# Grouping small float32 products by array shape in a two-block kernel on one core

## The chip, the cores and the metric

The kernel runs on one core of a Trainium2 chip. Its engines are TensorE (PE in the profile, with PEld for its weight loads), VectorE (DVE), ScalarE (ACT), GpSimd (POOL) and SyncE (SP, which mostly issues transfers). The metric is device microseconds of one launch; the median of several runs counts.

## The reference

Two blocks on x of [1024 tokens, 1024 channels], all in float32. Block 1: a mixer (half pooling, half a state-space model), then a SwiGLU layer. Block 2: attention and a gated recurrence side by side, then a squared-ReLU layer and a gate. The change touches the two recurrences only:

```python
def ssm_mixer(u, ...):            # 32 groups of 16 channels, 64 complex states each
    bu_r = jnp.einsum('blgh,gph->blgp', ug, bbar_r)     # and bu_i
    _, _, s_r, s_i = lax.associative_scan(_complex_affine_combine, (a_r, a_i, bu_r, bu_i), axis=1)
    y = einsum('blgp,ghp->blgh', s_r, c_re) - einsum('blgp,ghp->blgh', s_i, c_im) + d_skip * ug
    ...
def wkv7_scan(r, decay, k, v, a_vec, b_vec):            # 8 heads, state 64x64 each
    def step(state, inp):
        sa = jnp.einsum('bhvk,bhk->bhv', state, a_t)
        state = (state * d_t[:, :, None, :] + sa[..., None] * b_t[:, :, None, :]
                 + v_t[..., None] * k_t[:, :, None, :])
        return state, jnp.einsum('bhvk,bhk->bhv', state, r_t)
```

## The kernel before, in words

Large products split each operand into two parts of reduced precision and add three matmuls (lines L139 to L141, tile `big`); they make up most of the program. The two recurrences use plain float32 matmuls on small tiles, each of which stands in the trace as two matmul instructions. The source order is a suggestion: the framework's scheduler reorders instructions by readiness under its own costs, and each engine then runs its list strictly in that order.

**State-space mixer (block 1, about 115 to 240 us).** Four blocks b of 8 groups, chunks of 8 tokens. `ssm_taps(b)` makes, for each group g, two products into `pk` with a stationary operand of 128 rows by 16 columns (L413 with `c0`, L414 with `ca`) and a 128 by 128 transpose of `w` into `pt` (L415). DVE makes `c0` (L405); ACT copies `pk` to `ks` and `pt` to `bct` (L416, L417). `ssm_states(b)` makes for each group one product with 128 stationary columns into `pa` (L436) and two with 64 columns into the halves of `pb` (L437, L438); DVE multiplies `pa` (L439), then `pb` (L440), and scans. On PE `ssm_taps(b + 1)` follows `ssm_states(b)` directly, so L413 waits there for DVE's L405, which stands behind L439, two residual additions (L542) and L440. Between the blocks stand 24 large matmuls (`part_resid`) and `ssm_out`. The pool of `big` tiles has four buffers.

**Recurrence of block 2 (about 1300 to 1810 us).** Four time blocks tb of four chunks of 64 tokens. `wkv_prep(tb)` makes what does not need the state, the last of it the pair products (L1111): per chunk four products for the even heads (partitions 0 to 63) into one PSUM bank, four for the odd ones (64 to 127) into the other; DVE masks each bank into `at` (L1112), and SP stores its diagonal blocks. The pool `ps` has two banks. `wkv_inverse(tb)` loads these blocks and inverts them on DVE in 248 small steps over the four time blocks (L1140, L1141), stores and reloads the result, and finishes with products on PE (L1164, L1170). `wkv_chain(tb)` takes the four chunks one after the other: L1189 and L1190 (into `px`), a copy, L1195 (into `pu`), two copies, L1201 (update of the state), then for each of 8 heads the output as a sum of two products in place: L1204 (128 rows by 64 columns) and L1205 (64 by 64). DVE adds L1201's result to the state (L1207, L1208), but waits for the whole tile, L1205 included; the next chunk's L1190 needs that state. `wkv_chain(tb - 1)` is interleaved with `wkv_prep(tb)` and both with `wkv_inverse`. Large matmuls of the gate projections fill PE between them. L1018 (part of `head_rnorm`) needs a reciprocal of DVE (L1012).

Of the kernel before, what the change touches and what calls it, by code (L numbers as in the profile page):

```python
# [48 lines left out]
class Kernel:  # L49
# [49 lines left out]
    def split(self, x, hi, lo, scale=None):  # L99
        """hi + lo = x (or scale * x) exactly, each part of float32r's precision"""  # L100
        nc = self.nc
        if scale is None:
            nc.scalar.copy(hi, x)  # L103
            nc.vector.tensor_tensor(lo, x, hi.bitcast(F32), ALU.subtract)  # L104
        else:
            nc.scalar.activation(hi, x, AF.Identity, scale=scale)
            nc.vector.scalar_tensor_tensor(lo, x, scale, hi.bitcast(F32), ALU.mult, ALU.subtract)

    def half_pair(self, name):
        """hi and lo of [128, 512] in one slot"""  # L110
        t = self.slot(name, F32R)
        return t[:, 0:H], t[:, H:2 * H]

    def split_halves(self, x, name, scale=None):
        """The two token halves of [128, 1024], each with hi and lo in a slot of its own"""
        nc = self.nc
        out = [self.half_pair(name) for _ in range(2)]
        xs = [x[:, half * H:half * H + H] for half in range(2)]
        if scale is None:
            scale = 1.0  # L120
        for (hi, lo), xh in zip(out, xs):
            nc.scalar.activation(hi, xh, AF.Identity, scale=scale)
        for (hi, lo), xh in zip(out, xs):
            nc.vector.scalar_tensor_tensor(lo, xh, scale, hi.bitcast(F32), ALU.mult, ALU.subtract)
        return out
# [49 lines left out]
    def scaled(self, tiles):  # L175
        """The tiles with their rows scaled to a mean square of 1"""
        ss, xs = self.sumsq(tiles)
        rs = self.rsqrt(ss, len(tiles), 1.0 / D, EPS)
        for i, x in enumerate(tiles):
            self.nc.vector.tensor_scalar(xs[i], x, rs[:, i:i + 1], None, ALU.mult)  # L180
        return xs

    def norm_t_half(self, xs, g, out):
        """out: for each channel tile the hi and lo [128, 512] of g * xs, transposed"""
# [14 lines left out]
    def norm_t(self, res, g, groups=(3, 1), scaled=None):  # L199
        """The normalised input and what fills one half of it; scaled: the tiles, scaled already"""  # L200
# [15 lines left out]
    def units_steps(self, ws, x, nk=NK, w_off=0):  # L216
        """For each w: out[ch 128, tok 1024]; w: hi/lo [128, nk * 128], x[k][half]: hi/lo [128, 512]; a step for each half"""
# [11 lines left out]
    def norm_units(self, norm_half, x, ws):  # L229
        """norm_half(half) fills x[k][half]; the first units run between the halves"""  # L230
# [11 lines left out]
    def tok_matmul(self, x, w, evac):  # L242
        """out[tok 128, 1024 cols], x[k][half]: hi/lo [ch, tok 512], w: list of row blocks hi/lo [ch, 1024]"""
# [33 lines left out]
    def turns(self, out, phi, n):  # L277
        """out = (phi mod 2 pi) / (2 pi) in [-0.5, 0.5]"""
# [92 lines left out]
    def ssm_maps(self, b):  # L371
        """Input and output maps and rotations of the 8 groups of block b, from the parameters alone"""
# [5 lines left out]
        # input maps abar^j bbar (of token 7 - j of a chunk) and output maps C abar^(j + 1)  # L378
# [7 lines left out]
        # rotation by the angle of the chunk  # L386
# [11 lines left out]
    def ssm_taps(self, b, maps):  # L398
# [10 lines left out]
        # taps K[h, g, (tau, h')] of the convolution inside a chunk  # L409
        pk, pt = self.big(), self.big()  # L410
        g8 = lambda q: q.rearrange("p (g c) -> p g c", g=8)
        for g in range(8):
            nc.tensor.matmul(pk[0:16, g * P:g * P + 16], lhsT=w[:, g, 0:16], rhs=c0[:, g, :], start=True, stop=True)  # L413
            nc.tensor.matmul(pk[0:16, g * P + 16:(g + 1) * P], lhsT=w[:, g, 0:16], rhs=ca[:, g, 0:112], start=True, stop=True)  # L414
            nc.tensor.transpose(pt[:, g * P:(g + 1) * P], w[:, g, :], self.ident)  # L415
# [10 lines left out]
    def ssm_states(self, b, prep, ut):  # L426
        """States of block b at the ends of the chunks: rotated, then a real scan"""
# [6 lines left out]
        for g in range(8):  # L434
            sl = slice(g * P, (g + 1) * P)
            nc.tensor.matmul(pa[:, sl], lhsT=bct[:, g, :], rhs=ut[:, g, :], start=True, stop=True)  # L436
            nc.tensor.matmul(pb[0:64, sl], lhsT=bct[:, g, 64:128], rhs=ut[:, g, :], start=True, stop=True)  # L437
# [15 lines left out]
    def ssm_out(self, b, prep, states):  # L453
        """[ch 128, tok 1024] of block b"""
# [22 lines left out]
    def ssm_inputs(self, ps, b):  # L477
        """u^T [(g, h), tok] of 8 groups to DRAM as [(g, h), (j, c)] for tokens 8 c + j"""
# [5 lines left out]
    def ssm_load(self, b):  # L484
        """[(j 8, h 16), g 8, c 128], token 7 - j of chunk c"""
# [7 lines left out]
    def pool_diff(self, gi, pu):  # L493
        """Mean of the window minus the token"""
# [27 lines left out]
    def part_resid(self, mix, w_rows, src, dst):  # L522
        """dst = src + mix^T @ w, in steps"""
# [97 lines left out]
    def row_blocks(self, w, k0, n=4):  # L621
        """n row blocks of w from k0 on"""
        return [self.weights(w[(k0 + k) * P:(k0 + k + 1) * P, :], keep=True) for k in range(n)]

    def resid_matmul(self, mix, w, res):
        """res += mix^T @ w"""
# [9 lines left out]
    def ffn(self, res, g, chunks, up, act, w_down, last=lambda: None):  # L636
        """last: what goes between the last products; up: arrays of the weights that a tile of the hidden layer needs; act: what makes the tile of their products"""
# [40 lines left out]
    def block1(self, x2):  # L678
        """The rows of x2 go to DRAM; returns the normalised input of block 2 and what fills one half of it"""
# [10 lines left out]
        def scaled(ts):  # L690
            """Rows of rmsnorm(res) * g to x2, then scaled for the next norm"""
# [22 lines left out]

    def rope_tables(self):
        """[cos, cos, -sin, sin] over the 32 + 32 rotary rows (twice), and [sin rows | cos rows] of the keys"""
# [20 lines left out]
    def latents(self, cl, rs, rt):  # L737
        """hi and lo [ch, tok] of the two latents from DRAM with the gains of their norms, and the factors of the norms,
        which the products with them get: [tok 128, 8 tiles] and [128, tok]"""
# [22 lines left out]
    def heads(self, hp, out, psum, cq, ckv, kpe, cs, rq, rk):  # L762
        """Queries (with the scale of the softmax in them) and keys of a pair of heads to out, in 6 steps"""
# [28 lines left out]
    def attention(self, cq, ckv, rv, rq, rk):  # L792
        """hi and lo of the outputs [ch, tok] of each pair of heads"""
# [90 lines left out]
    def rope_keys(self, hn, w):  # L884
        """The rotary part of the keys and the table of the queries, to DRAM"""
# [12 lines left out]
    def rwkv_z(self, norm_half, hn):  # L898
        """Token-shifted projections: r, k, v go to DRAM; the low-rank inputs stay on chip"""
# [51 lines left out]
    def rwkv(self, hn):  # L951
        nc, a = self.nc, self.a
        # the diagonal blocks [time block, pair of chunks, block, head parity, chunk, head pair, row, column], then their inverses
# [34 lines left out]
    def per_pt(self, out, x, func, scale=1.0, bias=0.0):  # L988
        """One activation for each of the four head pairs, with its own column of scale and bias"""
# [4 lines left out]
    def head_sum(self, x):  # L994
        """Sums over the channels of each head, on all of its channels, in two banks of 2 head pairs"""
# [7 lines left out]
    def head_rnorm(self, x, scale, bias, floor):  # L1003
        """1 / max(sqrt(scale * (sum over a head) + bias), floor), on all channels of the head, in two banks"""
# [23 lines left out]
    def wkv_prep(self, tb, live):  # L1028
        """What the chunks of time block tb need apart from the state, in steps"""
# [13 lines left out]
        # normalised removal key  # L1043
# [11 lines left out]
        # even heads lie on partitions 0..63, odd ones on 64..127; the products of a pair of chunks have the  # L1055
        # rows of k before those of b for even heads, after them for odd ones
# [19 lines left out]
        # bonus  # L1076
# [8 lines left out]
        # token-major values (their mean over the head removed) and keys, pair products of each chunk  # L1085
        mask = self.cst[:, 744:872].unsqueeze(1).to_broadcast([P, 4, P])
        brow = (od, ev)
        for c2 in range(2):
# [16 lines left out]
            for c in range(2):  # L1105
                c4 = 2 * c2 + c
                at.append(self.slot("at").rearrange("p (e a t) -> p e a t", e=2, a=4))
                for e, rows in enumerate((ev, od)):
                    ps = self.ps()
                    for pt in range(4):  # L1110
                        nc.tensor.matmul(ps[:, pt * P:(pt + 1) * P], lhsT=bk[c2][rows, c, pt, :, :], rhs=ar[c2][rows, c, pt, :, :], start=True, stop=True)  # L1111
                    nc.vector.tensor_tensor(at[c4][:, e], ps.rearrange("p (a t) -> p a t", a=4), mask, ALU.mult)  # L1112
# [6 lines left out]
    def wkv_inverse(self, tb, live):  # L1119
        """Inverses of the 32 x 32 diagonal blocks by substitution, then of the 64 x 64 ones"""  # L1120
        nc = self.nc
        ar, at, bt, uv, bv, dp = live
        # partitions: pair of chunks, parity r of the row, block, head parity, chunk, head pair; row 2 k + r lies at k
# [32 lines left out]
        # T21 = T22 A21 T11  # L1156
# [17 lines left out]
    def wkv_chain(self, live):  # L1174
        """The chunks of a time block one after the other, a step for each"""
# [7 lines left out]
        for c in range(4):  # L1183
# [16 lines left out]
            for pt, e in hs:  # L1200
                nc.tensor.matmul(pg[half[e], pt * 64:pt * 64 + 64], lhsT=bt[c // 2][:, c % 2, pt, half[e]], rhs=u4[:, pt, e, :], start=True, stop=True)  # L1201
            for pt, e in hs:
                o = pg[half[e], 256 + pt * 64:320 + pt * 64]
                nc.tensor.matmul(o, lhsT=u4[:, pt, e, :], rhs=at[c][:, e, pt, 64:128], start=True, stop=False)  # L1204
                nc.tensor.matmul(o, lhsT=self.state[half[e], pt, :], rhs=ars(pt, e, 1), start=False, stop=True)  # L1205
# [7 lines left out]
    def wkv_out(self, tb, live):  # L1213
        """Group norm, bonus, gate"""
# [16 lines left out]
    def projections(self, hn):  # L1231
        """The gates and the latents before their norm, to DRAM, and the factors of the norms: [tok 128, 8 tiles of each]
        and [8 tiles of each, tok 128]"""
# [31 lines left out]
    def branch(self, w, x, g0, other=None, step=lambda i: None):  # L1265
        """gate * (x @ w); with other, hi and lo of its sum with that; step(i): what goes ahead of unit i"""
# [24 lines left out]
    def ple_inputs(self):  # L1291
        """hi and lo of p, transposed, and of its weights"""
# [12 lines left out]
    def ple_proj(self):  # L1305
        """p @ w_ple_proj, to DRAM"""
# [73 lines left out]
def layout(i):  # L1380
    """The arrays of setup_inputs() in the order in which the kernel reads them."""
# [114 lines left out]
```

## Time and profile before

| what | value |
|---|---|
| runs: median (lowest to highest) | 3104.06 us (3086.15 to 3108.91), 3 runs |
| profiled execution: span, first to last instruction | 3103.3 us (no other time of it is given) |
| PE busy | 2983.4 us, 96% |
| DVE busy, ACT busy | 1403.7 us (45%), 825.7 us (27%) |
| share of the chain that ended last | PE 88%, DVE 8%, ACT 2% |
| PE's largest group | L139, x1872 at 400 ns, 747.8 us |
| busy of L1204, all shapes | 42.9 us, x256 |

A matmul's duration in the trace overlaps with its neighbours'; what one costs is the distance from its start to the next start. A group that is merged in the timeline shows its first start, the time from there to its last end, and a count.

### The profile page before, as it was taken

How to read it: one execution, taken by the hardware profiler on the slowest of the kernel's cores; microseconds unless marked ns; L12 is line 12 of the kernel's file. 1: busy time of each engine (PE TensorE's matmuls, PEld its weight loads, DVE VectorE, ACT ScalarE, POOL GpSimd, SP SyncE). 2: the span in 40 equal slices, each digit the busy share in tenths (PEclk: the TensorE clock that was granted, in tenths of full speed). 3: DMA queues.
4: the chain of work that ended last, by engine and by line, in shares of the span. 5: the costliest groups of instructions: out<-in, count | busy, mean ns of one | idle time of the engine just before them, and what ended most of it. 6: DMA issues, size and time to landing. Idle time of an engine off the chain costs nothing.

```text
span 3103.3 us, 36712 instructions
## 1 busy us (share of the span) xinstructions
PE 2983.4 (96%) x15289; PEld 2374.1 (77%) x15289; DVE 1403.7 (45%) x2469; ACT 825.7 (27%) x1229; POOL 21.8 (1%) x73
## 2 busy tenths in 40 slices
PE   8999999999999999989879899999999999999998
PEld 6667888888888877767657677778788888888777
DVE  7665422222232551373664425645453333333356
ACT  4233311111111343232332133432231112221133
POOL 0000000000000000000000000000000000000000
PEclk9999999999999998987889899999999999999999
DMA  3334111111111333321323230013311111111122
GB/s 130 103 96 171 33 39 44 62 48 41 41 55 54 121 110 143 122 85 56 92 56 92 72 109 16 23 72 116 129 34 41 41 41 55 54 50 46 41 75 95
DMA packets 126389, 225.37 MB, mean 73 GB/s; under 512 B 52176, under 2 KB 73296, under 8 KB 126224
## 3 DMA queue, kind: packets, MB, share of 16 engines
q1 hardware_dynamic: 117200, 211.00, 20.5%
q10 hardware_dynamic: 9024, 12.04, 1.4%
q8 instruction: 120, 1.97, 0.3%
q14 instruction: 45, 0.37, 0.0%
HBM read 171.48 MB, written 48.23 MB: 71 GB/s over the span
## 4 chain that ended last, share of the span: by engine, by line
PE 88%; DVE 8%; ACT 2%; issue 1%; DMA 1%; SPq 0%; DVEq 0%; ACTq 0%
PE big L141 24%; PE big L139 24%; PE big L140 24%; PE big L819 2%; PE chain L852 2%; DVE tt L1141 2%; DVE wt L1140 2%; PE chain L1205 1%; PE chain L1204 1%; PE ps L1111 1%; PE ps L836 1%; PE ps L1018 1%; PE big L192 1%; PE chain L1201 0%; PE chain L1190 0%
## 5 line engine op out<-in xcount | busy, mean ns | idle before, releaser
L139 PE MATMUL big<-hn,wh 128*128 128x512 f32 x1872 | 747.8, 400 | 12.5 <-ACT zo L1256 5.7
L141 PE MATMUL big<-hn,wl 128*128 128x512 f32 x1872 | 747.9, 400 | 3.2 <-DVE wl L104 3.2
L140 PE MATMUL big<-hn,wh 128*128 128x512 f32 x1872 | 746.8, 399 | 1.9 <-DVE hn L197 1.9
L139 PEld LDWEIGHTS big<-hn,wh 128*128 128x128 f32 x1872 | 355.2, 190 | 99.3 <-ACT zo L1256 6.6
L141 PEld LDWEIGHTS big<-hn,wl 128*128 128x128 f32 x1872 | 355.1, 190 | 89.4 <-DVE wl L104 7.6
L140 PEld LDWEIGHTS big<-hn,wh 128*128 128x128 f32 x1872 | 355.3, 190 | 87.5 <-DVE hn L197 3.2
L103 ACT CAST wh<-wr 128x1024 fp32r<-128x1024 f32 (+1 forms) x142 | 142.0, 1001 | 966.1 <-PE big L140 734.1
L104 DVE TENSOR_TENSOR wl<-wr,wh 128x1024 fp32r<-128x1024 f32 (+1 forms) x142 | 165.1, 1162 | 408.2 <-ACT wh L103 403.5
L140 PE MATMUL big<-wk,a 128*128 128x512 f32 x864 | 339.0, 394 | 0.1
L141 PE MATMUL big<-wk,a 128*128 128x512 f32 x864 | 338.9, 394 | 0.0
L139 PE MATMUL big<-wk,a 128*128 128x512 f32 x864 | 335.3, 396 | 1.8 <-ACT wk L103 1.8
L656 DVE TENSOR_TENSOR r<-big,r 128x1024 f32<-128x1024 f32 x144 | 176.2, 1224 | 318.7 <-PE big L141 318.5
L139 PEld LDWEIGHTS big<-wk,a 128*128 128x128 f32 x864 | 161.2, 188 | 43.8 <-ACT wk L103 7.5
L140 PEld LDWEIGHTS big<-wk,a 128*128 128x128 f32 x864 | 162.8, 188 | 38.9 <-DVE wk L104 0.8
L141 PEld LDWEIGHTS big<-wk,a 128*128 128x128 f32 x864 | 162.7, 188 | 37.5
L671 ACT ACTIVATE zo<-big 128x1024 f32<-128x1024 f32 x32 | 32.8, 1026 | 369.6 <-PE big L141 369.5
L665 DVE TENSOR_TENSOR zo<-zo,big 128x1024 f32<-128x1024 f32 x22 | 26.9, 1221 | 204.3 <-PE big L141 204.3
L104 DVE TENSOR_TENSOR wk<-wr,wk 128x1024 fp32r<-128x1024 f32 (+1 forms) x86 | 100.3, 1172 | 30.9 <-ACT wk L103 30.8
L139 PE MATMUL big<-wk,mx 128*128 128x512 f32 x256 | 103.0, 409 | 2.9 <-ACT wk L103 2.9
L140 PE MATMUL big<-wk,mx 128*128 128x512 f32 x256 | 103.3, 404 | 1.0 <-DVE wk L104 1.0
L141 PE MATMUL big<-wk,mx 128*128 128x512 f32 x256 | 102.8, 401 | 0.0
L672 DVE TENSOR_TENSOR zo<-zo 128x1024 f32<-128x1024 f32 x32 | 39.2, 1225 | 131.2 <-ACT zo L671 131.2
(411 smaller groups left out, 3766.3 us busy)
## 6 DMA issues: line engine op xcount, KB each, us to landing
wr<-in_w_ffn_up_dram SPq DMA_DIRECT2D x32, 512.0 KB, 3.3
wr<-in_w_ffn_down_dram SPq DMA_DIRECT2D x32, 512.0 KB, 3.2
zr<-zo SPq DMA_DIRECT2D x24, 512.0 KB, 3.4
wr<-in_w_gate_dram SPq DMA_DIRECT2D x22, 512.0 KB, 3.3
wr<-in_w_up_dram SPq DMA_DIRECT2D x22, 512.0 KB, 3.3
wr<-in_w_down_dram SPq DMA_DIRECT2D x22, 512.0 KB, 3.3
wr<-in_w_gates_dram SPq DMA_DIRECT2D x16, 512.0 KB, 4.4
gd<-zo SPq DMA_DIRECT2D x16, 512.0 KB, 3.0
```

What stands on the lines that cost most here:

```text
L103: nc.scalar.copy(hi, x)
L104: nc.vector.tensor_tensor(lo, x, hi.bitcast(F32), ALU.subtract)
L139: nc.tensor.matmul(ps, lhsT=w[0], rhs=x[0], start=start, stop=False)
L140: nc.tensor.matmul(ps, lhsT=w[0], rhs=x[1], start=False, stop=False)
L141: nc.tensor.matmul(ps, lhsT=w[1], rhs=x[0], start=False, stop=stop)
L656: nc.vector.tensor_tensor(res[t], ps, res[t], ALU.add)
L671: nc.scalar.activation(s, ps, AF.Relu)
L672: nc.vector.tensor_tensor(s, s, s, ALU.mult)
L819: nc.tensor.matmul(sc[:, c:c + m], lhsT=qs[e][:, i * P:(i + 1) * P], rhs=ks[e][:, c:c + m], start=True, stop=True)
L852: nc.tensor.matmul(o, lhsT=pts[t // 4][:, (t % 4) * P:(t % 4 + 1) * P], rhs=vh, start=t == 0, stop=t == i)
L1140: nc.vector.tensor_tensor(t3, d[h, j:j + 1, j + 1:32].to_broadcast([64, n, m]), tt[h, 0:n, j:j + 1].to_broadcast([64, n, m]), ALU.mult)
L1141: nc.vector.tensor_tensor(tt[h, 0:n, j + 1:32], tt[h, 0:n, j + 1:32], t3, ALU.add)
```

## The change

Four places change; all comments and docstrings are gone too, so lines carry other numbers after the change (L1204 is L1208, L1205 is L1210, L1111 is L1114, L413 to L415 are L415, L416 and L413, L436 to L438 are L437, L440 and L441).

```diff
 ssm_taps:
         for g in range(8):
+            nc.tensor.transpose(pt[:, g * P:(g + 1) * P], w[:, g, :], self.ident)
+        for g in range(8):
             nc.tensor.matmul(pk[0:16, g * P:g * P + 16], lhsT=w[:, g, 0:16], rhs=c0[:, g, :], ...)
             nc.tensor.matmul(pk[0:16, g * P + 16:(g + 1) * P], lhsT=w[:, g, 0:16], rhs=ca[:, g, 0:112], ...)
-            nc.tensor.transpose(pt[:, g * P:(g + 1) * P], w[:, g, :], self.ident)
 ssm_states:
             nc.tensor.matmul(pa[:, sl], lhsT=bct[:, g, :], rhs=ut[:, g, :], start=True, stop=True)
+        for g in range(8):
+            sl = slice(g * P, (g + 1) * P)
             nc.tensor.matmul(pb[0:64, sl], lhsT=bct[:, g, 64:128], rhs=ut[:, g, :], start=True, stop=True)
 wkv_prep:
-                for e, rows in enumerate((ev, od)):
-                    ps = self.ps()
-                    for pt in range(4):
+                pair = [self.ps() for _ in range(2)]
+                for pt in range(4):
+                    for ps, rows in zip(pair, (ev, od)):
                         nc.tensor.matmul(ps[:, pt * P:(pt + 1) * P], lhsT=bk[c2][rows, c, pt, :, :], ...)
+                for e, ps in enumerate(pair):
                     nc.vector.tensor_tensor(at[c4][:, e], ps.rearrange("p (a t) -> p a t", a=4), mask, ALU.mult)
 wkv_chain:
+            out = lambda pt, e: pg[half[e], 256 + pt * 64:320 + pt * 64]
             for pt, e in hs:
-                o = pg[half[e], 256 + pt * 64:320 + pt * 64]
-                nc.tensor.matmul(o, lhsT=u4[:, pt, e, :], rhs=at[c][:, e, pt, 64:128], start=True, stop=False)
-                nc.tensor.matmul(o, lhsT=self.state[half[e], pt, :], rhs=ars(pt, e, 1), start=False, stop=True)
+                nc.tensor.matmul(out(pt, e), lhsT=u4[:, pt, e, :], rhs=at[c][:, e, pt, 64:128], start=pt == 0, stop=False, skip_group_check=True)
+            for pt, e in hs:
+                nc.tensor.matmul(out(pt, e), lhsT=self.state[half[e], pt, :], rhs=ars(pt, e, 1), start=False, stop=True, skip_group_check=True)
```

On PE, the outputs of the first chunk of the recurrence, before (the eight pairs go on as they begin):

```order
L1201 MATMUL chain_8710<-uv_8260,bt_8282 64x64 x7
L1204 MATMUL chain_8710<-at_8295,uv_8260 64x64
L1205 MATMUL chain_8710<-ar_8228,wkv_s_8180 64x64
L1204 MATMUL chain_8710<-at_8295,uv_8260 64x64
L1205 MATMUL chain_8710<-ar_8228,wkv_s_8180 64x64
L1204 MATMUL chain_8710<-at_8295,uv_8260 64x64
L1205 MATMUL chain_8710<-ar_8228,wkv_s_8180 64x64
```

and in the change:

```order
L1205 MATMUL chain_8710<-uv_8260,bt_8282 64x64 x7
L1208 MATMUL chain_8710<-at_8295,uv_8260 64x64 x8
L1210 MATMUL chain_8710<-ar_8228,wkv_s_8180 64x64 x8
L1193 MATMUL chain_8808<-uv_8260,at_8312 64x64
L1098 MATMUL ps_8868<-cst,v_8617 64x64 x15
```

The state update, the first and the second products of the outputs now stand in three uninterrupted runs, here and in nearly all of the 16 chunks. The first run now opens its accumulation (`start`) with the first head of each half only.

On PE, the pair products of two chunks of time block 0 as the change has them (`ps_8296` and `ps_8313` are the even heads' banks):

```order
L1114 MATMUL ps_8296<-ar_8228,bk_8238 128x128 x4
L1114 MATMUL ps_8297<-ar_8228,bk_8238 128x128 x4
L1114 MATMUL ps_8313<-ar_8228,bk_8238 128x128 x4
L1114 MATMUL ps_8314<-ar_8228,bk_8238 128x128 x4
```

and of one chunk of time block 1:

```order
L1114 MATMUL ps_8903<-ar_8610,bk_8620 128x128
L1114 MATMUL ps_8904<-ar_8610,bk_8620 128x128
L1114 MATMUL ps_8903<-ar_8610,bk_8620 128x128
L1114 MATMUL ps_8904<-ar_8610,bk_8620 128x128
```

The scheduler left four and four in 11 of the 16 chunks; the source's alternation stands in full in one chunk, with other work between in a second, and in part in three more.

On DVE, the end of the second inverse (tiles `wt`, `tt`) and the preparation of time block 2 (`rn`, `kk`, `km`, `a`), before:

```order
L1140 TENSOR_TENSOR wt_1232_9104<-d_9093,tt_9094 64x16
L1011 TENSOR_SCALAR rn_9310<-rn_9310 128x256
L1141 TENSOR_TENSOR tt_9094<-tt_9094,wt_1232_9104 64x16
L157 TENSOR_TENSOR t_11427<-t_11423,t_11425 128x16
L1012 RECIPROCAL rn_9310<-rn_9310 128x256
L1144 COPY tt_9094<-tt_9094 128x512
```

and in the change:

```order
L1015 RECIPROCAL rn_9310<-rn_9310 128x256
L1144 TENSOR_TENSOR wt_1232_9104<-d_9093,tt_9094 64x45
L1069 TENSOR_TENSOR ar_9332<-r_9330,P_9292 128x4x2x64
L1145 TENSOR_TENSOR tt_9094<-tt_9094,wt_1232_9104 64x15x3
L158 TENSOR_TENSOR t_11427<-t_11427,t_11423 128x16
L104 TENSOR_TENSOR wl_11562<-wr_11559,wh_11561 128x1024
L1144 TENSOR_TENSOR wt_1232_9104<-d_9093,tt_9094 64x30
L1053 TENSOR_TENSOR kk_9298<-kk_9298,ps_9314 128x512
L1145 TENSOR_TENSOR tt_9094<-tt_9094,wt_1232_9104 64x15x2
L1053 TENSOR_TENSOR kk_9298<-kk_9298,ps_9317 128x512
L1144 TENSOR_TENSOR wt_1232_9104<-d_9093,tt_9094 64x16
L1056 TENSOR_TENSOR km_9299<-km_9299,k_9296 128x1024
```

Work that stood behind the second inverse now stands between its last steps.

## Rows read from the trace of the kernel before

**Rows 1.** From the page: the span, and the chain that ended last by engine.

```profile
span 3103.3 us, 36712 instructions
...
PE 88%; DVE 8%; ACT 2%; issue 1%; DMA 1%; SPq 0%; DVEq 0%; ACTq 0%
```

**Rows 2.** Windows: stretch, length, busy per engine, PEclk (1.00 is full), DMA share, GB/s.

```profile
115.00:240.00 125.00, 113.44 (x733) 82.90 (x732) 80.30 (x111) 36.88 (x42) 3.89 (x12) 0.89 0.41 108
...
1350.00:1800.00 450.00, 394.69 (x3360) 299.66 (x3358) 258.83 (x702) 129.79 (x217) 3.30 (x17) 0.88 0.25 74
...
1400.00:1450.00 50.00, 50.00 (x544) 40.44 (x543) 12.28 (x26) 9.18 (x24) 1.01 (x5) 0.67 0.22 62
```

**Rows 3.** Timeline of PE in one chunk: start, us to last end, line, tiles, count.

```profile
1785.02 0.68 PE L1195 MATMUL chain<-xs,at 64*64 64x64 f32 x16
...
1787.21 0.62 PE L1201 MATMUL chain<-uv,bt 128*64 128x64 f32 x13
1787.62 0.22 PE L1204 MATMUL chain<-at,uv 128*64 128x64 f32 x1
...
1787.83 0.33 PE L1205 MATMUL chain<-ar,wst 64*64 64x64 f32 x2
1788.08 0.33 PE L1204 MATMUL chain<-at,uv 128*64 128x64 f32 x2
...
1791.53 0.22 PE L1205 MATMUL chain<-ar,wst 64*64 64x64 f32 x1
```

**Rows 4.** Timeline of DVE where the second inverse begins; brackets: idle before, releaser.

```profile
1455.41 0.42 DVE L1207 TENSOR_TENSOR wst<-chain,wst 128x256 f32<-128x256 f32 x1 [7.41 <-PE chain L1205]
...
1456.21 0.17 DVE L1140 TENSOR_TENSOR wt<-d,tt 64x31 f32<-64x31 f32 x1
```

**Rows 5.** Waits of PE from 1320 to 1830 us: total, times, longest.

```profile
PE ps L1018 <- DVE rn L1012: 40.0, 5, 11.2
```

**Rows 6.** Timeline of DVE just after the last step of the second inverse.

```profile
1508.41 1.75 DVE L1012 RECIPROCAL rn<-rn 128x256 f32<-128x256 f32 x1
...
1511.44 0.69 DVE L1050 TENSOR_TENSOR kk<-kk,ps 128x512 f32<-128x512 f32 x1
1512.04 1.22 DVE L1053 TENSOR_TENSOR km<-km,k 128x1024 f32<-128x1024 f32 x1
```

**Rows 7.** Timeline of PE: pair products of two chunks.

```profile
1325.55 3.82 PE L1111 MATMUL ps<-ar,bk 64*128 64x128 f32 x32
```

**Rows 8.** Timeline of PE: the first taps, and transposes of the recurrence for comparison.

```profile
122.45 0.22 PE L413 MATMUL big<-sb_bct,sb_w 128*16 128x16 f32 x2
122.52 0.35 PE L414 MATMUL big<-sb_ca,sb_w 128*16 128x112 f32 x2
122.80 0.33 PE L415 MATMUL big<-cst,sb_w 128*128 128x128 f32 x1
...
127.11 0.48 PE L139 MATMUL big<-wk,mx 128*128 128x512 f32 x1
...
1427.24 0.66 PE L1103 MATMUL ps<-cst,bk 128*128 128x128 f32 x4
```

**Rows 9.** Timeline of PE: first and last rows of the states of blocks 0 and 1.

```profile
132.79 0.38 PE L436 MATMUL big<-ut,sb_bct 128*128 128x128 f32 x2
...
138.78 0.27 PE L438 MATMUL big<-ut,sb_bct 128*64 128x128 f32 x1
...
162.72 1.95 PE L436 MATMUL big<-ut,sb_bct 128*128 128x128 f32 x16
...
166.29 0.27 PE L438 MATMUL big<-ut,sb_bct 128*64 128x128 f32 x1
```

**Rows 10.** Timeline of DVE, then PE: what stands between states and the next taps.

```profile
138.72 1.23 DVE L439 TENSOR_TENSOR sb_v<-big,sb_ang 128x1024 f32<-128x1024 f32 x1 [1.34 <-PE big L436]
...
142.61 0.21 PE L413 MATMUL big<-sb_bct,sb_w 128*16 128x16 f32 x2 [3.56 <-DVE sb_bct L405]
...
196.07 0.21 PE L413 MATMUL big<-sb_bct,sb_w 128*16 128x16 f32 x2 [2.27 <-DVE sb_bct L405]
```

## The prediction, written before the change was run

> **What bounds the kernel now.** I began with the page. The span is 3103.3 us and PE carries 88% of the chain that ended last, DVE 8% [rows 1]; so a microsecond taken from PE is worth a microsecond unless PE only waits longer somewhere. The span is 0.8 us under the median of the runs, so sums against it need no correction. Next the windows of the two recurrences. Between 1350 and 1800 us PE is busy 394.69 of 450 us, DVE 258.83, at a mean granted clock of 0.88; between 115 and 240 us PE is busy 113.44 of 125 at 0.89 [rows 2]. PE is the bound in both, not by much: the places where it waits for DVE decide what a saving is worth. Two views name them. In the waits the five stops of L1018 for DVE's reciprocal take 40.0 us, the longest 11.2 [rows 5]; in the timeline of block 1, L413 stops 3.56 us, and later 2.27, for DVE's L405 [rows 10].
>
> **Chunk outputs (L1204, L1205).** In one chunk the sixteen products, a pair of instructions each, run from 1787.62 to 1791.53 plus 0.22, which is 4.13 us, 0.258 per pair [rows 3]. From the first L1205 at 1787.83 to the next L1204 at 1788.08 its two instructions take 0.25 us. The same engine runs other small products of one shape far faster: L1201, with the same 128 rows and 64 columns as L1204, 13 in 0.62 us, where the last lasts 0.22, so (0.62 - 0.22) / 12 = 0.033 us a step; and L1195, with the 64 by 64 of L1205, 16 in 0.68 us [rows 3]. The grouped order in the program is exactly such runs. So the first products, 16 instructions, should take 16 x 0.033 = 0.53, the change of shape about 0.15 (the 0.258 of a pair less some 0.11 for the two instructions of one shape), the second products 0.68: 1.36 us instead of 4.13, 2.77 saved in each chunk, 44 us in 16 chunks.
>
> The Trainium skill has a rule against this. Its page "TensorE: Matmul & The Clock Gate", section "Part 3: Packing small matmuls", says that a weight load overlaps running matmuls only where its row group differs; L1204's operand fills all rows, so its weights could not hide and grouping would give little. The trace disagrees on the rows of the same shape: L1201 also fills 128 rows and takes 0.033 us a step [rows 3]. I go by the row and keep the rule as a rival.
>
> How much lies on the path? DVE's state update waits for the whole tile, L1205 included, so each chunk's outputs delay the next chunk. The four inverses run on DVE beside the chain of the block before. The second inverse's first step starts at 1456.21, 0.4 us after the state update that begins at 1455.41 and that had waited 7.41 us for L1205 [rows 4]. So what the three chunks before it save brings the inverse forward, and with it all that hangs on it; the third and fourth inverse stand so too. That makes nine chunks, and the four of the last block, after which no inverse comes, make thirteen: 13 x 2.77 = **-36 us**. The other three chunks (8.3 us) lie under the inverse, whose length on DVE does not change: there PE only reaches L1018 earlier and waits longer [rows 5]. Bounds: four chunks alone, -11; all sixteen, -44.
>
> **Pair products (L1111).** They take 0.12 us each, 32 in 3.82 [rows 7]. The scheduler leaves four and four in 11 of 16 chunks, where nothing changes. In the other five chunks even and odd heads alternate wholly or in part. I know no row with this alternation. If it halved them, 16 instructions x 0.06 = 0.95 us a chunk would go, -4 in all after allowing for the partial ones; if a bank held twice as long cost a wait of the length of a DVE operation (0.69, [rows 6]) in each of the five, +4. I take 0, because the pool has only two banks and the mask waits for the same last product either way.
>
> **Taps (L413 to L415).** The first taps run from 122.45 to 127.11, 4.66 us with a change of shape at every step [rows 8]. Grouped, sixteen transpose instructions go at the pace of L1103's four in 0.66, (0.66 - 0.33) / 3 = 0.11, so 1.4 to 1.8; the narrow products alternate between 16 and 112 columns but keep one stationary operand shape, some 2 us: 3.3, a saving of 1.35. In taps 1 to 3 the products wait for L405 [rows 10], and the transposes, which need no L405, now fill that wait; behind it stand about 2.2 us instead of 4.66: 3 x 2.4 = -7.2.
>
> **States (L436 to L438).** Here the trace holds both orders. The states of block 0 stand alternating: 132.79 to 138.78 + 0.27, 6.26 us. In block 1 the scheduler had grouped them already: 162.72 to 166.29 + 0.27, 3.84 [rows 9]. So 2.4 us each for blocks 0, 2 and 3. In block 0 the next taps wait for DVE, which idles only 1.34 us before L439 [rows 10], so only those 1.34 count; in blocks 2 and 3 I take the whole, -4.8. Block 1 so far: 1.35 + 1.34 + 7.2 + 4.8 = -14.7. Its mean clock of 0.89 over 125 us means 125 x 0.11 x 2 = 27 us at 1.2 GHz instead of 2.4 [rows 2], and the low stretches follow the waits at L413; as those get filled I add an estimated -4 of the 13.7 us that they cost: **-19 us**. Bounds: -10 if DVE stays the limit behind the states of blocks 2 and 3 and the clock gives nothing, -26 if two thirds of that clock loss go.
>
> **DVE's order in the second inverse.** Preparation of time block 2 moves ahead of the last steps: the reciprocal 1.75, two `kk` and one scaling at 0.69 each, `km` 1.22 [rows 6], 5.0 us later for the inverse's end. But the reciprocal then also releases L1018 earlier, and the same work stood between this inverse and the next chunk's copies, where PE has large matmuls to run. Net 0, bounds +5 and -5.
>
> **Sum:** 3103.3 - 36 - 19 = **3048 us**, and 3032 to 3065 with the bounds taken together in part.
>
> **Rivals.**
> A, the DVE period holds: the inverses wait for something else as soon as the chain no longer delays them (the `ks` of a preparation, the L1018 stop), and nine chunks' savings turn into longer stops at L1018. For it: those stops take 40.0 us already [rows 5]. Against it: the 0.4 us of [rows 4]. Only four chunks count: 3103.3 - 19 - 11 = 3073. Chance 0.18.
> B, the clock comes back: between 1400 and 1450 PE is busy for the whole 50 us at a mean of 0.67, so 33 us ran at 1.2 GHz and cost 16 [rows 2]. It follows stretches of small alternating products; if dense runs remove it, -16 there and another -8 in block 1: 3024. Against it: a shorter run of small products leaves PE idle sooner. Chance 0.12.
> C, grouped runs don't overlap. Then a step costs 0.11 us, as within a shape now, 16 x 0.11 = 1.76 instead of 0.53: 13 x 1.23 = 16 us less gain, 3064. Against it: L1201 at 0.033. Chance 0.04; the rule quoted above would give this.
> E, the cost isn't the alternation but adding into the bank written just before; the outputs then gain nothing: 3103.3 - 19 = 3084. Against it: the states, where no product adds to another, shrink by grouping alone [rows 9]. Chance 0.03. Of the same kind is the Trainium skill's "TensorEngine Tiling (Array Packing)", section "Gotcha 1: PSUM Pressure": different row tiles can't use one PSUM bank at once, and L1205 alternates halves into one bank. The trace disagrees: L1195 alternates halves into one bank too and has 16 in 0.68 us [rows 3].
> D, slower: PE finishes its small products sooner, stands idle longer at L1018, and the granted clock behind each stop falls. Some 350 us of PE work in the window remain; at a mean of 0.67, as in the worst stretch [rows 2], they take 350 x (0.88 / 0.67 - 1) = 110 us more, less the 55 gained: 3158; the middle of this case is 3138. It decides from a mean below 0.76, where 350 x (0.88 / 0.76 - 1) = 55 eats the whole gain. For it: 1400 to 1450 shows that the engine can be busy at 0.67. Chance 0.03, since the stops grow by 8 us at most. My forecast keeps 0.60.
>
> **How the numbers follow.** The time is that of the forecast, 3048. The range 3018 to 3080 takes in A, C and most of B and leaves out E and D and the tails. A measurement tells some 1%, 31 us, from no change. Faster by more than that: forecast, B, C and half of A, 0.60 + 0.12 + 0.04 + 0.09 = 0.85. Within 1%: half of A and E, 0.12. Slower: D, 0.03.
>
> **What would show it.** In PE's timeline two runs of about 0.5 to 0.7 us for each chunk's outputs (C: 1.8; E: as now 4); states of block 0 in about 3.8 us; taps 1 to 3 with transposes ahead of the wait; in the waits L1018's stops 8 us longer (A: 30 us longer); the second inverse's first step some 8 us earlier against its preparation; the mean clocks of the three windows near 0.88, 0.9 and 0.67 (B: above 0.8 in the last; D: below 0.8 in the first). I am wrong if the outputs shrink as said and the inverses still start as late after one another as now.

## The result, and the profile after

| | before | after |
|---|---|---|
| median of the runs (lowest to highest) | 3103.64 us (3086.15 to 3108.91), 4 runs | 3023.71 us (3020.11 to 3026.19), 4 runs |
| profiled execution, span | 3103.3 us | 3023.3 us |
| ratio after / before, 95% interval | | 0.9745 (0.9719 to 0.9772) |

The change is 80 us faster. The forecast was 3048 us, 55 less than before, in a range of 3018 to 3080. The page of the changed kernel, as in [rows 1]:

```profile
span 3023.3 us, 36716 instructions
...
PE 87%; DVE 9%; issue 2%; ACT 1%; DMA 1%; ACTq 0%; SPq 0%; DVEq 0%
```

PE still bounds it. Where the 80 us went is read from windows that are cut at the same events in both traces: the state-space stretch (first taps to last output product), then alternately the stretch behind an inverse on DVE, up to the next inverse, which is called a chain here (chain 0 to chain 3), and that next inverse (the second to the fourth). First before (start and end, length, busy time and instructions of PE, PEld, DVE, ACT, POOL, then PEclk, DMA share, GB/s; the first row is the state-space stretch, then chain 0, the second inverse, chain 1, the third, chain 2, the fourth, chain 3):

```profile
122.40:237.40 115.00, 104.34 (x689) 75.55 (x688) 78.88 (x108) 35.04 (x40) 3.46 (x9) 0.88 0.42 112
...
1391.40:1456.20 64.80, 62.77 (x618) 49.40 (x617) 21.42 (x40) 13.01 (x30) 1.01 (x5) 0.72 0.22 55
1456.20:1508.30 52.10, 40.66 (x236) 29.46 (x236) 43.85 (x146) 23.24 (x32) 0.13 (x1) 0.85 0.20 65
1508.30:1575.30 67.00, 66.93 (x678) 51.72 (x677) 31.28 (x57) 16.63 (x34) 1.01 (x5) 0.96 0.33 92
1575.30:1626.90 51.60, 36.56 (x209) 26.40 (x209) 42.18 (x141) 19.05 (x28) 0.13 (x1) 0.82 0.18 55
1626.90:1692.50 65.60, 64.33 (x678) 49.65 (x677) 30.92 (x50) 20.05 (x39) 1.02 (x5) 1.00 0.35 102
1692.50:1741.20 48.70, 36.13 (x215) 27.14 (x214) 40.28 (x136) 11.38 (x16) 0.00 (x0) 0.86 0.19 63
1741.20:1802.40 61.20, 61.20 (x628) 45.05 (x627) 10.89 (x23) 11.41 (x21) 0.00 (x0) 0.97 0.24 68
```

and the changed kernel in the same order:

```profile
122.30:218.30 96.00, 85.81 (x690) 74.69 (x688) 78.68 (x108) 34.77 (x39) 3.46 (x9) 0.95 0.51 134
...
1373.50:1416.50 43.00, 40.95 (x621) 32.22 (x620) 21.28 (x40) 12.98 (x30) 1.01 (x5) 0.96 0.33 82
1416.50:1471.80 55.30, 39.28 (x238) 28.61 (x237) 49.05 (x153) 23.26 (x32) 0.13 (x1) 0.81 0.29 91
1471.80:1523.30 51.50, 50.67 (x653) 39.71 (x652) 26.13 (x51) 16.33 (x34) 1.01 (x5) 1.00 0.29 77
1523.30:1569.90 46.60, 33.91 (x224) 25.19 (x223) 41.96 (x140) 18.42 (x27) 0.13 (x1) 0.89 0.24 74
1569.90:1626.30 56.40, 54.38 (x676) 42.54 (x674) 31.34 (x50) 20.57 (x41) 1.01 (x5) 1.00 0.38 110
1626.30:1674.00 47.70, 35.48 (x224) 27.33 (x224) 40.24 (x135) 11.44 (x15) 0.00 (x0) 0.86 0.23 76
1674.00:1722.60 48.60, 48.60 (x628) 36.66 (x627) 10.84 (x22) 11.40 (x21) 0.00 (x0) 1.00 0.25 66
```

The state-space stretch is 19.0 us shorter. The four chains are 21.8, 15.5, 9.2 and 12.6 shorter, and of the inverses the second is 3.2 longer, the third 5.0 and the fourth 1.0 shorter: 61.9 us from the end of the first inverse to the last output. Together that is 80.9; what lies between the two stretches takes 1.2 us more, and what follows them is unchanged (1300.9 and 1300.7 us). The largest piece, chain 0, is also the one in which the clock moved most, from 0.72 to 0.96.

One chunk's outputs in PE's timeline of the changed kernel, in the place of [rows 3]:

```profile
1712.95 0.62 PE L1205 MATMUL chain<-uv,bt 128*64 128x64 f32 x13
1713.36 0.22 PE L1208 MATMUL chain<-at,uv 128*64 128x64 f32 x1
...
1713.42 0.68 PE L1208 MATMUL chain<-at,uv 128*64 128x64 f32 x15
1714.03 0.51 PE L1210 MATMUL chain<-ar,wst 64*64 64x64 f32 x10
...
1714.43 0.28 PE L1210 MATMUL chain<-ar,wst 64*64 64x64 f32 x3
```

From 1713.36 to 1714.43 + 0.28 it is 1.35 us, where there were 4.13 [rows 3]. In the state-space part the first taps and the states of block 0, in the place of [rows 8] and [rows 9]:

```profile
122.47 1.03 PE L413 MATMUL big<-cst,sb_w 128*128 128x128 f32 x8
123.43 0.22 PE L415 MATMUL big<-sb_bct,sb_w 128*16 128x16 f32 x2
...
125.47 0.50 PE L139 MATMUL big<-wk,mx 128*128 128x512 f32 x1
...
131.14 1.95 PE L437 MATMUL big<-ut,sb_bct 128*128 128x128 f32 x16
...
134.71 0.27 PE L441 MATMUL big<-ut,sb_bct 128*64 128x128 f32 x1
```

The taps take 3.0 us instead of 4.66, the states 3.84 instead of 6.26. Of the waits on PE (total, times, longest) that of the taps for L405 is now 2.9 us in three stops, where it was 7.9 (3.56 at the first alone, [rows 10]), but two stops are new: the states (L437) for a residual addition and the transposes (L413) for DVE's L442, which was L439. L1018, now L1021, waits about as long as in [rows 5]:

```profile
PE big L437 <- DVE r L545: 3.0, 1, 3.0
PE big L415 <- DVE sb_bct L405: 2.9, 3, 1.4
PE big L413 <- DVE sb_v L442: 2.0, 1, 2.0
...
PE ps L1021 <- DVE rn L1015: 43.0, 6, 10.9
```

### The profile page after: what moved, and what is told of

Same layout as the page of the kernel before. It is cut to its first block, busy times and chain, and to the rows that moved or that the text cites. A ratio compares the mean times of both kernels' runs of the same rounds, so it can differ in the third digit from the quotient of the medians.

```text
span 3023.3 us, 36716 instructions
## 1 busy us (share of the span) xinstructions
PE 2899.8 (96%) x15289; PEld 2327.6 (77%) x15289; DVE 1404.1 (46%) x2469; ACT 825.3 (27%) x1229; POOL 21.8 (1%) x73
## 4 chain that ended last, share of the span: by engine, by line
PE 87%; DVE 9%; issue 2%; ACT 1%; DMA 1%; ACTq 0%; SPq 0%; DVEq 0%
PE big L139 24%; PE big L140 24%; PE big L141 24%; PE big L822 2%; PE chain L855 2%; DVE tt L1145 2%; DVE wt L1144 2%; PE ps L839 1%; PE ps L1114 1%; PE ps L1021 1%; PE big L192 1%; PE chain L1205 0%; PE chain L139 0%; PE chain L140 0%; PE chain L141 0%
```

## The experiments

**Each part alone.** Theory 1 said that the outputs carry the recurrence of block 2 and its clock; theory 2 that the clock came back through the shift from block 1 or through the pair products. The outputs alone, in the kernel before (long arguments are cut to `...` in all excerpts):

```diff
 for pt, e in hs:
-    o = pg[half[e], 256 + pt * 64:320 + pt * 64]
-    nc.tensor.matmul(o, lhsT=u4[:, pt, e, :], ..., start=True, stop=False)
-    nc.tensor.matmul(o, lhsT=self.state[half[e], pt, :], ..., start=False, stop=True)
+    nc.tensor.matmul(out(pt, e), lhsT=u4[:, pt, e, :], ..., start=pt == 0, stop=False, skip_group_check=True)
+for pt, e in hs:
+    nc.tensor.matmul(out(pt, e), lhsT=self.state[half[e], pt, :], ..., start=False, stop=True, skip_group_check=True)
```

> Only the sixteen chunk outputs are grouped; taps, states and pair products as before. The changed kernel is 80 us faster; its trace puts 62 of them between the first inverse and the last chunk. Theory 1 (the outputs alone carry that stretch: 2.77 us less in each chunk on the path, and the granted clock there recovers because of it): 55 to 62 us faster, 3042 to 3049, and the mean granted clock between the first and the second inverse above 0.9. Theory 2 (the outputs give their 36 us, and the clock of the stretch recovers only together with the shift that block 1 brings or with the pair products): 32 to 40 us faster, about 3067, and the clock between the first and the second inverse stays near 0.72.

Measured: 3040.87 us, ratio 0.9816 (0.9791 to 0.9841), beside a median of 3101.70 for the kernel before. The changed kernel with this edit taken back:

> The changed kernel with the outputs put back to alternating pairs. Theory 1 (outputs carry the stretch): 18 to 25 us faster than before, about 3082. Theory 2 (the clock comes back with the shift of block 1 or the pair products): 40 to 48 us faster, about 3060, with the clock between the first and the second inverse above 0.9 though the outputs alternate.

Measured: 3078.78 us, 0.9942 (0.9923 to 0.9962). Taps and states alone (the first two parts of the change's diff):

> Only taps and states are grouped. Theory 1: 18 us faster as in the changed kernel's trace of that stretch, 3085, and nothing after it changes. Theory 2: about 15 us more, from the clock in the recurrence of block 2, 3070.

Measured: 3085.70 us, 0.9949 (0.9925 to 0.9973). The pair products alone (its third part):

> Only the order of the pair products is changed; it alternates in the same few chunks as in the changed kernel. In its trace a chunk that alternates in full takes 1.0 us for 16 instructions instead of 1.8. Theory 1: 0 to 5 us faster, 3099 to 3104. Theory 2 (they also keep the clock up): 10 us or more faster, and the clock between the first and the second inverse above 0.8. A third possibility, two banks held at once, would make it slower by up to 4 us.

Measured: 3097.96 us, 0.9991 (0.9972 to 1.0010), no difference that can be told. The four medians agree with theory 1: beside 3101.70 the outputs alone give 61 us, block 1 alone 16, the pair products alone at most a few, and block 1 with the pair products 23. What the outputs do to the stretch shows in one window of each trace, from the end of the first inverse to the last output; the outputs alone:

```profile
1388.10:1740.20 352.10, 308.63 (x3253) 236.91 (x3251) 220.59 (x587) 114.61 (x196) 3.29 (x17) 0.93 0.28 82
```

all but the outputs:

```profile
1371.90:1778.80 406.90, 363.90 (x3253) 275.17 (x3251) 220.81 (x587) 114.24 (x196) 3.30 (x17) 0.89 0.25 74
```

taps and states alone:

```profile
1372.30:1780.10 407.80, 369.06 (x3253) 279.38 (x3251) 220.85 (x587) 114.94 (x196) 3.31 (x17) 0.89 0.25 73
```

and the kernel before:

```profile
1391.40:1802.40 411.00, 368.58 (x3253) 278.83 (x3251) 220.83 (x588) 114.78 (x196) 3.30 (x17) 0.89 0.25 73
```

With the same instructions, wherever the outputs alternate the stretch takes 406 to 411 us at a mean clock of 0.89 or 0.90; with grouped outputs 352 at 0.93. Theory 2's clock of chain 0 did rise without the grouped outputs in the two kernels that have the new pair products (0.92 with them alone, 0.88 in all but the outputs), but in both chain 1 fell from 0.96 to 0.85, and their whole stretches take 405.8 and 406.9 us: the low clock moved from one stretch to another, and the sum fell by 4 to 5 us only.

**Why alternating costs.** Two kernels keep the alternation of the kernel before. In one the second product replaces the first in place of adding to it, so the first is missing from its result:

```diff
-    nc.tensor.matmul(o, lhsT=u4[:, pt, e, :], ..., start=True, stop=False)
-    nc.tensor.matmul(o, lhsT=self.state[half[e], pt, :], ..., start=False, stop=True)
+    nc.tensor.matmul(o, lhsT=u4[:, pt, e, :], ..., start=True, stop=True)
+    nc.tensor.matmul(o, lhsT=self.state[half[e], pt, :], ..., start=True, stop=True)
```

> The kernel before, with its alternating outputs, but the second product of each pair overwrites the first instead of adding to it (the first product is left out of the result). Theory 1 (what costs is the change from a 128-row to a 64-row stationary operand): a chunk's outputs still take 4.1 us and the time stays at 3102. Rival E of the prediction (adding into what was just written costs): a chunk takes 1.4 us and the time falls by 55 to 62 us.

In the other both products have 128 rows:

```diff
-    nc.tensor.matmul(o, lhsT=self.state[half[e], pt, :], rhs=ars(pt, e, 1), start=False, stop=True)
+    nc.tensor.matmul(o, lhsT=self.state[:, pt, :], rhs=ar[c // 2][:, c % 2, pt, 1, :], start=False, stop=True)
```

> The kernel before with the same alternation and the same adding in place, but the second product takes all 128 rows of the state and of its right side, so that both products have the shape 128 rows by 64 columns (each output then contains the other head's second product too). Theory 1: without a change of shape a chunk takes 32 x 0.033 = 1.1 us to 1.4, and the time falls by 55 to 62 us. Rival E: it stays at 4.1 us a chunk and 3102 us. Rival C of the prediction (no overlap between weight loads of equal row groups): 32 x 0.11 = 3.5 us a chunk and about 3090.

The first takes 3102.77 us, 1.0005 (0.9979 to 1.0032); PE's timeline within one chunk:

```profile
1783.98 0.33 PE L1205 MATMUL chain<-ar,wst 64*64 64x64 f32 x2
1784.23 0.33 PE L1204 MATMUL chain<-at,uv 128*64 128x64 f32 x2
1784.49 0.32 PE L1205 MATMUL chain<-ar,wst 64*64 64x64 f32 x2
```

0.255 us per pair as ever. The second takes 3047.24 us, 0.9835 (0.9789 to 0.9881; two runs), 52 us less than the 3099.38 beside it and so a little less than the 55 to 62 expected, and there the timeline reads

```profile
1736.40 0.27 PE L1204 MATMUL chain<-at,uv 128*64 128x64 f32 x2
1736.46 0.22 PE L1205 MATMUL chain<-ar,wst 128*64 128x64 f32 x1
1736.51 0.22 PE L1204 MATMUL chain<-at,uv 128*64 128x64 f32 x1
...
1737.22 0.33 PE L1205 MATMUL chain<-ar,wst 128*64 128x64 f32 x3
```

The eight pairs of products run from 1736.34 to 1737.55, 1.2 us, still alternating and still adding in place. So in the outputs the cost is the change of shape from 128 rows to 64 and back, not the order and not the sum: rival E is out, and so is C, since 32 instructions that all take the 128 rows start 0.032 us apart on average ((1.21 - 0.22) / 31). The stretch's clock comes back with it: its window from the end of the first inverse to the last output is

```profile
1389.80:1745.60 355.80, 310.90 (x3253) 239.24 (x3252) 220.69 (x589) 114.77 (x196) 3.31 (x17) 0.92 0.28 81
```

**Taps against states.** The taps alone (the first part of the diff):

> Only the taps are grouped, the states alternate. The state-space stretch (first taps to last output product) took 115 us before and 96 when both are grouped. Theory 1 (the taps give 1.35 in the first block and 2.4 in each of the three others, and a share of the clock): 103 to 106 us; the time 8 to 12 us lower, 3090 to 3094. If the states carried most of the gain: 110 us or more.

Measured: 3089.97 us, 0.9971 (0.9945 to 0.9998), and in its trace 104.3 us for the state-space stretch at a clock of 0.92:

```profile
122.00:226.30 104.30, 95.14 (x690) 76.85 (x688) 78.64 (x108) 34.99 (x39) 3.46 (x9) 0.92 0.47 123
```

So the taps give 10.7 of the 19.0 us and the states, by difference, the other 8.3; the states were not run alone.

**The pair products in every chunk.** The changed kernel with both halves in one tile of two banks (the masks read from there):

```diff
-pair = [self.ps() for _ in range(2)]
+pair = self.big()
 ...
-        nc.tensor.matmul(ps[:, pt * P:(pt + 1) * P], ...)
+        nc.tensor.matmul(pair[:, (4 * e + pt) * P:(4 * e + pt + 1) * P], ...)
```

> The changed kernel with the pair products of even and odd heads written to the two banks of one large tile, so that they alternate in all 16 chunks, not in 5. Theory 1: 0.8 us less in each of eleven more chunks, of which those on the path (the first block's four and the last two blocks' in part) count: 3 to 9 us faster than the changed kernel, 3015 to 3021. Rival (the large tile is missed by the large matmuls, which have only two): 5 to 20 us slower than the changed kernel, 3029 to 3044.

Measured: 3129.43 us, 1.0101 (1.0065 to 1.0137): slower than both, and by more than the rival said. One of its waits between 1280 and 1860, and its window from 1300 to 1850:

```profile
PE ps L1021 <- DVE rn L1015: 102.0, 6, 27.1
```

```profile
1300.00:1850.00 550.00, 398.14 (x3730) 312.45 (x3731) 288.32 (x763) 141.61 (x245) 3.32 (x17) 0.82 0.25 74
```

The pair tiles come out of the pool of two tiles that the large products use. Between 1281.5 and 1580.1 no large product of the gate projections starts, the last pair product at 1577.6; in the changed kernel they fill PE beside the inverses from 1293.6 on. So PE stands 102 us at L1021 instead of 43 and is busy for 398 of 550 us, at a clock of 0.82; in 550 us of the changed kernel (1280 to 1830) it is 487, at 0.93. And the pair products without their change, in the changed kernel:

> The changed kernel with the pair products put back to four even, four odd; outputs, taps and states grouped. Theory 1 (outputs and block 1 carry all of it, the pair products in five chunks are worth 0 to 4 us): 3024 to 3028. If the pair products had cost more by the order that they give DVE in the second inverse (54.3 us in the changed kernel, 52.1 before, 48.0 with the outputs alone) than they give PE: 3018 to 3022, faster than both kernels.

Measured: 3029.61 us, 0.9764 (0.9739 to 0.9789), a little above both expectations; it overlaps with the changed kernel's 0.9719 to 0.9772, so that no difference can be told. In its trace the second inverse takes 49.0 us and chain 1 57.1, against 55.3 and 51.5 in the changed kernel.

**A further step.** Writing the grouped outputs elsewhere (and copying them out from there), so that DVE's state update doesn't wait for them:

```diff
-out = lambda pt, e: pg[half[e], 256 + pt * 64:320 + pt * 64]
+out = lambda pt, e: pu[half[e], 256 + pt * 64:320 + pt * 64]
```

> The changed kernel with the grouped outputs written to the free half of pu instead of the tile of the state update. DVE's state update then waits for the run of L1205 alone and not for the outputs (1.4 us a chunk); it is the wait through which the outputs reached the path. If the state update is still what the chain and the inverse wait for: up to 16 x 1.3 = 20 us less than the changed kernel, 3004 to 3015. If PE, busy for all but 1 or 2 us of each stretch between two inverses, is the bound there by now: 0 to 6 us less, 3018 to 3024.

> The changed kernel itself, beside the last one on the same chip: 3020 to 3027.

Measured: 3018.93 us, 0.9736 (0.9707 to 0.9765), beside 3020.66, 0.9746 (0.9720 to 0.9772), for the changed kernel: no difference that can be told. DVE's state updates now idle 19.2 us in all, for L1205, where they idled 24.7 for L1210: most of what was left of that wait was not for the outputs. Chain 3 is the clearest:

```profile
1676.50:1720.00 43.50, 43.50 (x607) 33.05 (x605) 10.37 (x23) 9.42 (x19) 0.00 (x0) 1.00 0.37 113
```

PE is busy for all of it, as it was in the 48.60 of the changed kernel; the 5 us fewer hold 607 instructions instead of 628, and the whole run is no shorter by a measurable amount. The scheduler placed other work anew as well: the second inverse takes 50.2 us here and chain 1 57.9, against 55.3 and 51.4 in the kernel beside it.

## Why the prediction was right, and where its size was off

**The sum.** Block 1 gave the 19 us of the forecast, though its terms did not, so that the match is partly luck. The recurrence of block 2 gave 61.9 where 36 were forecast. Of the 26 us between, some 8 are the three chunks that I had called hidden, and some 18 the clock. The time lies in the range because the range had been drawn to take in most of rival B. Of the signs, the runs of the outputs and the states came as said; the second inverse came 21.8 us earlier behind the first instead of 8, L1018's stops grew by 3 us instead of 8, and the clocks of the three windows were 0.92, 0.96 and 0.97 (the last shifted to 1380 to 1430), as rival B had them.

**Outputs, size of one chunk.** Right: 2.77 us forecast, 4.13 - 1.35 = 2.78 found. The row on L1201 was the one to go by. The rule of the Trainium skill (page "TensorE: Matmul & The Clock Gate", section "Part 3: Packing small matmuls") that a weight load overlaps running matmuls only where its row group differs, which I had kept as rival C, is not what limits these products: with all rows in use throughout, the 32 instructions of a chunk run in 1.2 us.

**Outputs, how many chunks count.** This is a step that was off. I took thirteen and said that the fourth chunks of the first three time blocks lie under an inverse "whose length on DVE does not change". But on DVE the state update of that chunk stands in the middle of the inverse's steps, and while DVE waits there the inverse stands still. In DVE's timeline of the kernel before, with its wait, and the inverse's next step behind it:

```profile
1585.74 0.42 DVE L1207 TENSOR_TENSOR wst<-chain,wst 128x256 f32<-128x256 f32 x1 [2.23 <-PE chain L1205]
1586.19 0.22 DVE L1140 TENSOR_TENSOR wt<-d,tt 64x58 f32<-64x58 f32 x1
```

and of the changed kernel, with none:

```profile
1531.55 0.42 DVE L1212 TENSOR_TENSOR wst<-chain,wst 128x256 f32<-128x256 f32 x1
```

The three such waits were 1.94, 2.23 and 2.23 us and are now 0.28, 0 and 0.35: 5.8 us that I had called hidden. In the kernel with the outputs alone, where the preparation has not moved into the second inverse (146 DVE instructions in it, as before, not 153), the three inverses take

```profile
1432.30:1481.00 48.70, 36.61 (x231) 27.07 (x230) 43.74 (x146) 23.23 (x32) 0.13 (x1) 0.82 0.22 70
...
1539.00:1587.10 48.10, 33.48 (x208) 24.19 (x207) 42.12 (x141) 18.91 (x28) 0.13 (x1) 0.82 0.19 59
...
1644.80:1691.20 46.40, 33.33 (x213) 25.20 (x213) 40.20 (x136) 11.32 (x15) 0.00 (x0) 0.85 0.20 66
```

instead of 52.1, 51.6 and 48.7. So nearly all sixteen chunks are on the path, 16 x 2.77 = 44 us, the upper bound of my term. DVE's idle time before all its state updates (total, times) points the same way, before

```profile
PE chain L1205: 70.0, 16
```

and in the changed kernel

```profile
PE chain L1210: 24.7, 13
```

which is 45 us less.

**The clock.** This term was the most mis-sized. I gave it 4 us, in block 1 alone, and left chain 0 to rival B with a chance of 0.12. Over the stretch from the first inverse's end to the last output it went from 0.89 of 411.0 us to 0.93 of 349.1:

```profile
1373.50:1722.60 349.10, 303.28 (x3253) 232.25 (x3251) 220.84 (x588) 114.40 (x196) 3.30 (x17) 0.93 0.29 83
```

A mean clock of 0.89 loses 0.11 of the time in which PE is busy. That makes, as an estimate, 411.0 x 0.11 - 349.1 x 0.07 = 21 us (rather less, since PE idles in part of it), most of it in chain 0, where 64.8 x 0.28 - 43.0 x 0.04 = 16 us come back. With the 44 of the outputs that makes 65 for the 61.9 found. The two overlap: in chain 0 of the kernel before, the first chunk's outputs ran wholly at a clock of 0.50 and took 6.47 us (1416.74 to 1423.21), not 4.13, so part of what the clock cost lies in the outputs themselves. In block 1 the same estimate gives 115.0 x 0.12 - 96.0 x 0.05 = 9 us, not 4. My argument against rival B, that a shorter run of small products leaves PE idle sooner, did not decide: L1021 waits 43.0 us instead of 40.0, and the clock rises all the same. Rival B's 3024 was nearly the time, partly by luck: its clock in the recurrence came, but its further 8 us in block 1 did not (19.0, not 27), and the chunks that I had called hidden made up for them.

**Block 1.** The sum was right, 19 us; its parts were not quite: taps 10.7 and states 8.3, clock included, and up to 9 of the 19 may be clock where I had 4. The sixteen transpose instructions of the prediction are eight, since a transpose stands in the trace as one instruction and not as two; they take 1.03 us, and the first taps gave 1.66 us rather than 1.35. That the transposes fill the wait did not shorten PE's idle time: the stops for L405 fell from 7.9 us to 2.9, but the new stops at L437 and L413 took 5.0. PE idles 10.7 us of the 115.0 before and 10.2 of the 96.0 after; 18.5 of the 19.0 us came out of its busy time. The narrow products of the second taps still ran at a clock of 0.50 after their wait (139.5 to 143.1); before, the whole second taps did, and took 7.6 us (142.6 to 150.2), not the 4.66 that I had counted for them. My bound of 26 for block 1 does not follow from its terms either: 14.7 and two thirds of 13.7 make 24.

**Pair products and DVE's order.** Right in the sum, 0. An alternating chunk does run as fast as my lower bound, as this pair of chunks in PE's timeline shows, the first alternating in full, the second in part:

```profile
1405.52 1.16 PE L1114 MATMUL ps<-ar,bk 64*128 64x128 f32 x16
...
1407.84 1.49 PE L1114 MATMUL ps<-ar,bk 64*128 64x128 f32 x16
```

with 3.82 / 2 = 1.9 us for one in the old order [rows 7]; there are too few of them to count. The new order on DVE comes from this part too: the second inverse takes 55.3 us with it and 49.0 in the changed kernel without it, 6.3 more, slightly over my bound of 5, and chain 1 takes 51.5 instead of 57.1, 5.6 less. What is moved ahead of the inverse's end is not done behind it.

**Rival D** was a true mechanism in the wrong kernel: longer stops at L1021 and a falling clock are what made the kernel with the large pair tile slower. Rival A fell: with the outputs shortened, the inverses do start sooner after one another, as here after the third chunk (in the place of [rows 4]; the second inverse follows at 1416.53):

```profile
1415.72 0.42 DVE L1212 TENSOR_TENSOR wst<-chain,wst 128x256 f32<-128x256 f32 x1 [2.84 <-PE chain L1210]
```

What stays open is why the clock is lower with alternating products: whether the slow steps themselves or the time that the stretch takes lets it fall. The runs show only that the kernels with grouped outputs or with one shape have it at 0.92 to 0.94 over the stretch, and all with alternating outputs at 0.89 or 0.90. The one exception has grouped outputs and the large pair tile: 0.77 over its stretch, in which PE is busy for 216 of 318 us.

## What to carry to other kernels

Look in the timeline for small products whose starts are several times as far apart as those of a neighbour of the same shape, and put products of one stationary shape next to each other, or give them one shape; the sum in place may stay. Before calling a wait hidden under another engine's work, look whether its consumer stands in the middle of that engine's list. When small products get denser, allow for the granted clock as a term of the sum, and read its cost from the stretch in which it is lowest. And compare an engine's idle time over a whole stretch before counting a shortened wait as gained: another stop can take its place.

## What was not expected of the hardware

Products of 128 rows by 64 columns follow one another at 0.03 us even when they add to the address just written, while at a change between 128 and 64 rows the next instruction starts 0.15 us later and even the second instruction of a pair then starts 0.11 after the first; at half the clock such a pair took 0.40 us instead of 0.26. Alternating even and odd heads, rows 0 to 63 and 64 to 127, into two banks brings an instruction from 0.11 to 0.06 us; the runs do not tell the rows from the banks. And in the kernels with alternating outputs the mean granted clock of a stretch of some 400 us was steadier (0.89 or 0.90 in all) than that of its first part, chain 0, in which it went from 0.72 to 0.92.
